# Recurrent block of a two-layer trunk: gate products as 64-row pairs one step later, and the high parts of 12 of 16 input weight tiles loaded by casting transfers

## The chip, the cores and the metric

The kernel runs on one core of one Trainium2 chip. A core has TensorE (PE in the profile, with its weight loads PEld), VectorE (DVE), ScalarE (ACT), GpSimd (POOL), SyncE (SP, which here only issues transfers), and 16 DMA engines that move data between HBM and the on-chip memory. Products are accumulated in PSUM, which has eight banks of 128 partitions by 512 float32. The metric is the device time of one execution in microseconds; before the change the median of three runs is 1560.44 us (1560.33 to 1563.29).

## The reference

A trunk of two layers on 512 positions and 1024 channels. Each layer is half a feed-forward block, a token mixer, and another half feed-forward block; the mixer of layer 0 is recurrent, that of layer 1 a gated spatial one. The change touches the recurrent mixer alone:

```
def rg_lru(x, w_a, b_a, w_x, b_x, lam):
    gate_a = sigmoid(block_diag_linear(x, w_a, b_a))      # 16 heads of 64 x 64
    gate_x = sigmoid(block_diag_linear(x, w_x, b_x))
    log_a = -8.0 * gate_a * softplus(-lam)
    a = exp(log_a);  mult = sqrt(-expm1(2.0 * log_a))
    h[t] = a[t] * h[t-1] + x[t] * gate_x[t] * mult[t]     # a scan over positions

def recurrent_mixer(x, w_in, ...):
    y, r = split(x @ w_in, 2)                             # w_in: 1024 x 2048
    r = causal_depthwise_conv(r, conv_w, conv_b)          # 4 taps
    return (gelu(y) * rg_lru(r, ...)) @ w_out
```

## The kernel before, in words

**Split products.** Float32 products are made of three fast ones: each operand is split into a high part `hi`, which ACT writes by a copy into the float32r type, and a low part `lo`, which DVE writes as operand minus `hi`. The product is hi*hi + hi*lo + lo*hi (`mm3`, L245). For activations the helper `split` does it (its copy shows as L117 of ACT, its subtraction as L108 of DVE, like all uses of these two helpers); for weights the class `Sub` does, into the tiles `whi` and `wlo` of a pool with four buffers of each.

**Steps.** All work is a list `subs` of steps; one step is one weight tile and its products. The loop at the end of `trunk` goes through them in order. In step i it splits the weight tile of step i + 3, runs hooks in the phases `pre`, `mid` and `rest`, issues loads (`load_more`), emits the products, then runs `end`, the step's own `post`, and `late`. So the order of each engine's queue is the order in which this loop emits, and the numbers in hooks and plans set it.

**Weight buffers.** Raw weight tiles of 512 KB are loaded by SP into ten buffers (`RAW_BUFS`, tag `raw`). `load_more` loads on as long as fewer than ten tiles are `live`; a tile stops being live once its low part is written. The output projections use a fast scheme of seven products for eight block products, so most of their weight tiles get a second block added in place by POOL transfers that accumulate (L159).

**The recurrent mixer** (L1201 on). Let c0 to c7 be the eight tiles of 128 channels of r, and y0 to y7 those of y. Products in order: first halves (256 positions) of c0 to c3, then their second halves with the same weights, then c4 to c7 and y0 to y7 with 512 positions each, then the output projection. After each tile of r (`r_post`): ACT copies it from its bank with scale and bias (`rc`), DVE adds three taps, one step later ACT and DVE split the result, and at the end of step g PE makes the two gates (`gate`). The gate weights of two heads lie as a block diagonal in 128 x 128, the rest filled with zeros, so a gate is one `mm3` of 128 rows, into a bank of its own. In step g + 1 ACT takes both banks by sigmoids and makes a tanh (`tl`); in step g + 2 DVE multiplies r with its gate (`pr`). `plan` then places, relative to the first y step y0: exponentials, `a2` and `tl` arithmetic, square roots, scans, the gelu of y, and the product of both (`yh`), which makes the left operand of the output projection in blocks of two tiles (`a` in the profile). The blocks and their sums are split again. The output projection's product groups go in the order P1, P5, P2 for the first pair of row blocks, then the same for the second, into the banks A, C, B.

Of the kernel before, what the change touches and what calls it, by code (L numbers as in the profile page):

```python
# [35 lines left out]
SPLIT_AHEAD = 3  # L36
SLOTS = 56


# [34 lines left out]
def trunk(ctx: ExitStack, tc: tile.TileContext, a: dict, out: bass.AP):  # L74
# [57 lines left out]
    class Raw:  # L132


        halves = False

# [35 lines left out]
    class Sub:  # L172
# [1028 lines left out]
    def recurrent(w_in, w_out, norm):  # L1201
        gates = {}

        def load_gate(name, q):
            g = gates[name, q] = slot(name="gw")
            nc.gpsimd.memset(g, 0.0)
            gv = g.rearrange("p (c j) -> p c j", c=4)
            wv = a[f"rec_gate_{name}_w"][0, q * 8 : (q + 1) * 8].rearrange("(c two) i j -> two i c j", two=2)
            for two in range(2):
                nc.sync.dma_start(out=gv[two * 64 : (two + 1) * 64, :, two * 64 : (two + 1) * 64], in_=wv[two])  # L1210

        def split_gate(name, q):
            gates[name, q] = split(gates[name, q])

        at0 = len(subs)
        y0 = at0 + 12
        for n, (name, q) in enumerate((name, q) for q in range(2) for name in ("a", "x")):
            hook(at0 + (-9,-8,-2,-1)[n], "late", lambda name=name, q=q: load_gate(name, q))
            hook(at0 + (-3,-2,3,4)[n], "mid", lambda name=name, q=q: split_gate(name, q))

        rc, ga, gx, tl, pr, ym = {}, {}, {}, {}, {}, {}

        def r_post(c, ps):
            n = now[0]
            g = n + (2 if c < 4 or c == 6 else 1)
            v = rc[c] = slot(name="rc")
# [7 lines left out]
            def gate():  # L1234
                for name in "ax":
                    pg = bank("gate")
                    wh, wl = gates[name, c // 4]
                    cs = slice((c % 4) * P, (c % 4 + 1) * P)
                    mm3(pg, wh[:, cs], wl[:, cs], hl[0], hl[1], True, True)
                    pss.append(pg)  # L1240
                hl.clear()

            def sigmoids():
                for dst, brow in ((ga, V_GA), (gx, V_GX)):
                    dst[c] = slot(name="g")
                    act(dst[c], pss.pop(0), AF.Sigmoid, bias=vcol(brow + c))
                tl[c] = slot(name="tl")
# [6 lines left out]
            hook(n, "late", taps)  # L1254
            hook(n + 1, "mid", lambda: hl.extend(split(v)))
            hook(g, "end", gate)
# [84 lines left out]
        def mk(c0, post, halves):  # L1341

            raw = raw_of(w_in[:, c0 : c0 + P].rearrange("(k p) c -> p k c", p=P), [P, KD, P])
            st = {}

# [8 lines left out]

            last = lambda: post(st[0])
            if not halves:
# [294 lines left out]
    def vec_rest():  # L1651

        nc.vector.memset(stage[:V_ROWS, :P], 0.0)
        for src, r0, n in rows:
            flat = src.rearrange("h d -> (h d)") if len(src.shape) == 2 else src.rearrange("o h d -> (o h d)")
            nc.gpsimd.dma_start(out=stage[r0 : r0 + n, :P], in_=flat.rearrange("(n p) -> n p", p=P))

# [148 lines left out]
```

## Time and profile before

| | us |
|---|---|
| median of three runs | 1560.44 |
| the profiled execution | 1560.53 |
| its span in the trace | 1558.5 |
| PE busy | 1550.6 |
| DVE busy | 1309.5 |
| ACT busy | 1194.2 |
| POOL busy | 244.5 |
| recurrent products (first r product to first product of the output projection) | 329.46 to 430.50 |

Times within the span are microseconds from its start. Matmuls overlap: one of 512 columns is listed with 0.39 us, but the next starts 0.23 us later, so the start-to-start distance is what a product costs. Likewise an instruction of ACT or DVE starts up to 0.1 us before the one ahead of it ends. A row of the timeline may hold several instructions (x2, x3). The square bracket at its end is the idle time ahead of it and who ended it.

### The profile page before, as it was taken

How to read it: one execution, taken by the hardware profiler on the slowest of the kernel's cores; microseconds unless marked ns; L12 is line 12 of the kernel's file. 1: busy time of each engine (PE TensorE's matmuls, PEld its weight loads, DVE VectorE, ACT ScalarE, POOL GpSimd, SP SyncE). 2: the span in 40 equal slices, each digit the busy share in tenths (PEclk: the TensorE clock that was granted, in tenths of full speed). 3: DMA queues.
4: the chain of work that ended last, by engine and by line, in shares of the span. 5: the costliest groups of instructions: out<-in, count | busy, mean ns of one | idle time of the engine just before them, and what ended most of it. 6: DMA issues, size and time to landing. Idle time of an engine off the chain costs nothing.

```text
span 1558.5 us, 20998 instructions
## 1 busy us (share of the span) xinstructions
PE 1550.6 (99%) x7277; PEld 1317.1 (85%) x7277; DVE 1309.5 (84%) x1784; ACT 1194.2 (77%) x1785; POOL 244.5 (16%) x220
## 2 busy tenths in 40 slices
PE   9999999999999999999999999999999999999998
PEld 7888888898888998888889988888888889888886
DVE  6977789888999787789897877798979997777998
ACT  7877786668778868786787777867987877777856
POOL 2111112300021111112211111122211111111120
PEclk9999999999999999999999999999999999999999
DMA  9888898953395888899987887999978869898994
GB/s 316 187 189 192 188 219 223 232 142 108 98 236 136 191 198 198 187 235 223 232 209 180 191 203 185 230 218 235 252 191 216 203 140 218 197 206 184 241 232 137
DMA packets 272987, 311.58 MB, mean 200 GB/s; under 512 B 115456, under 2 KB 153456, under 8 KB 272880
## 3 DMA queue, kind: packets, MB, share of 16 engines
q1 hardware_dynamic: 218592, 211.06, 46.9%
q0 software_dynamic: 52496, 97.33, 37.1%
q10 hardware_dynamic: 1792, 1.84, 0.4%
q8 instruction: 57, 0.93, 0.2%
q14 instruction: 50, 0.41, 0.1%
HBM read 282.39 MB, written 2.10 MB: 183 GB/s over the span
## 4 chain that ended last, share of the span: by engine, by line
PE 98%; DVE 2%; DMA 0%; issue 0%; ACT 0%; DVEq 0%
PE A L483 15%; PE A L482 15%; PE A L481 15%; PE C L483 8%; PE C L481 8%; PE C L482 8%; PE B L482 4%; PE B L483 4%; PE B L481 4%; PE r L247 2%; PE r L248 2%; PE r L246 2%; PE Q L483 1%; PE Q L481 1%; PE Q L482 1%; PE p L961 1%
## 5 line engine op out<-in xcount | busy, mean ns | idle before, releaser
L108 DVE TENSOR_TENSOR wlo<-raw,whi 128x1024 fp32r<-128x1024 f32 (+2 forms) x567 | 651.1, 1152 | 210.6 <-ACT whi L117 207.0
L117 ACT ACTIVATE whi<-raw 128x1024 fp32r<-128x1024 f32 (+2 forms) x567 | 564.5, 1001 | 229.2 <-DVE raw L108 93.3
L481 PE MATMUL A<-whi,hi 128*128 128x512 f32 (+1 forms) x1104 | 420.8, 381 | 0.0
L482 PE MATMUL A<-whi,lo 128*128 128x512 f32 (+1 forms) x1104 | 419.3, 380 | 0.2 <-DVE lo L108 0.2
L483 PE MATMUL A<-wlo,hi 128*128 128x512 f32 (+1 forms) x1104 | 419.3, 380 | 0.0
L481 PEld LDWEIGHTS A<-whi,hi 128*128 128x128 f32 x1104 | 207.3, 188 | 35.9 <-ACT c L117 1.0
L482 PEld LDWEIGHTS A<-whi,lo 128*128 128x128 f32 x1104 | 207.3, 188 | 35.6 <-DVE lo L108 0.6
L483 PEld LDWEIGHTS A<-wlo,hi 128*128 128x128 f32 x1104 | 207.2, 188 | 35.7
L159 POOL DMA_DIRECT2D raw<-in_ffn_w_in_dram x100 | 120.7, 1207 | 708.8 <-DVE raw L108 322.8
L481 PE MATMUL C<-whi,hi 128*128 128x512 f32 (+1 forms) x608 | 231.5, 381 | 0.0
L483 PE MATMUL C<-wlo,hi 128*128 128x512 f32 (+1 forms) x608 | 231.3, 380 | 0.0
L482 PE MATMUL C<-whi,lo 128*128 128x512 f32 (+1 forms) x608 | 231.3, 380 | 0.0
L159 POOL DMA_DIRECT2D raw<-in_ffn_w_out_dram x73 | 83.8, 1189 | 319.0 <-DVE wlo L108 204.3
L108 DVE TENSOR_TENSOR raw<-raw,raw 128x1024 f32<-128x1024 f32 (+1 forms) x113 | 130.9, 1158 | 1.1
L482 PEld LDWEIGHTS C<-whi,lo 128*128 128x128 f32 x608 | 114.2, 188 | 20.2
L483 PEld LDWEIGHTS C<-wlo,hi 128*128 128x128 f32 x608 | 114.1, 188 | 19.9
L481 PEld LDWEIGHTS C<-whi,hi 128*128 128x128 f32 x608 | 114.1, 188 | 19.8
L117 ACT ACTIVATE c<-A 128x512 f32<-128x512 f32 (+1 forms) x150 | 81.8, 567 | 46.6 <-PE A L483 46.4
L108 DVE TENSOR_TENSOR lo<-a,hi 128x512 fp32r<-128x512 f32 (+1 forms) x180 | 116.3, 653 | 0.7 <-ACT hi L117 0.7
L117 ACT ACTIVATE hi<-a 128x512 fp32r<-128x512 f32 (+1 forms) x180 | 105.5, 596 | 14.4 <-DVE a L108 12.6
L482 PE MATMUL B<-whi,lo 128*128 128x512 f32 (+1 forms) x304 | 115.8, 381 | 0.0
L481 PE MATMUL B<-whi,hi 128*128 128x512 f32 (+1 forms) x304 | 115.7, 381 | 0.0
(190 smaller groups left out, 1973.5 us busy)
## 6 DMA issues: line engine op xcount, KB each, us to landing
raw<-in_ffn_w_in_dram SPq DMA_DIRECT2D x143, 512.0 KB, 5.5
raw<-in_ffn_w_out_dram SPq DMA_DIRECT2D x98, 512.0 KB, 5.7
raw<-in_ffn_w_in_dram POOLq DMA_DIRECT2D x76, 512.0 KB, 7.5
raw<-in_ffn_w_out_dram POOLq DMA_DIRECT2D x58, 512.0 KB, 8.4
raw<-in_ffn_w_in_dram SPq DMA_DIRECT2D x48, 384.0 KB, 4.0
raw<-in_sg_w_in_dram SPq DMA_DIRECT2D x20, 512.0 KB, 8.6
raw<-in_ffn_w_in_dram POOLq DMA_DIRECT2D x24, 384.0 KB, 6.4
raw<-in_rec_w_in_dram SPq DMA_DIRECT2D x16, 512.0 KB, 5.3
```

Source lines behind the costliest of these rows:

```text
L108: nc.vector.tensor_tensor(out=o, in0=x, in1=y, op=op)
L117: nc.scalar.activation(out=o, in_=x, func=f, **k)
L159: nc.gpsimd.dma_start(out=self.v, in_=src, accum_op=ALU.add)
L246: nc.tensor.matmul(ps, wh, xh, start=start, stop=False)
L247: nc.tensor.matmul(ps, wh, xl, start=False, stop=False)
L248: nc.tensor.matmul(ps, wl, xh, start=False, stop=stop)
L481: nc.tensor.matmul(ps, zh, wh, start=fresh and i == 0, stop=False, **k)
L482: nc.tensor.matmul(ps, zl, wh, start=False, stop=False, **k)
L483: nc.tensor.matmul(ps, zh, wl, start=False, stop=end, **k)
L961: nc.tensor.matmul(bank_of(half, s), z, (sub.lo if m == 2 else sub.hi)[:, q, :], start=left[2] == "2" and (h, q, m) == (0, 0, 0), stop=lef ...
```

## The change

**Gates.** The weights of gate a and gate x of two heads now share one 128 x 128 tile: on rows 0 to 63 the first head's a and x side by side, on rows 64 to 127 the second head's x and a. There are no zeros to fill, and two gate tiles are loaded and split where there were four. A gate step is three pairs of products; the first of a pair contracts rows 0 to 63, the second rows 64 to 127, each into a bank of its own with 128 output partitions. Each bank then holds half of gate a and half of gate x, and ACT takes them with four sigmoids of 64 partitions where it took two of 128. For that the bias of gate x is loaded with its halves exchanged. The table `GATE` sets the gate step: 3 steps behind the tile for c0 to c3 and 2 for c4 to c7, where it was 2 for c0 to c3 and c6, and 1 for c4, c5 and c7.

**Weights.** For c4 to c7 and y0 to y7 a tile is loaded twice: raw by SP as before, and into a second buffer of the raw pool by POOL with a cast to float32r. That second tile is the high part; ACT's copy falls away, DVE's subtraction stays. Its buffer is live until the products of its step are emitted. Such a tile needs two free buffers to be loaded.

**Plan.** Some exponentials, square roots and scans stand half a step to one step later.

```diff
+GATE = (3, 3, 3, 3, 2, 2, 2, 2)
...
             self.fetch()
+            if self.cast:
+                self.h = rawp.tile([P, 1024], F32R, tag="raw", name=nm("rawhi")).rearrange("p (k c) -> p k c", k=k)
+                live.add((self, "hi"))
+                nc.gpsimd.dma_start(out=self.h, in_=self.src)
...
             src = self.raw.v
+            if self.raw.cast:
+                self.hi = self.raw.h
+                _, k, c = src.shape
+                self.lo = wp.tile([P, 1024], F32R, tag="wlo", name=nm("wlo")).rearrange("p (k c) -> p k c", k=k)
+                tt(self.lo, src, f32(self.hi), ALU.subtract)
+                self.raw.used()
+                return
...
-        def load_gate(name, q):
-            g = gates[name, q] = slot(name="gw")
-            nc.gpsimd.memset(g, 0.0)
+        def load_gate(q):
+
+            g = gates[q] = slot(name="gw")
             gv = g.rearrange("p (c j) -> p c j", c=4)
...
+            for n, name in enumerate("ax"):
+                wv = a[f"rec_gate_{name}_w"][0, q * 8 : (q + 1) * 8].rearrange("(c two) i j -> two i c j", two=2)
+                for two in range(2):
+                    o = (two ^ n) * 64
+                    nc.sync.dma_start(out=gv[two * 64 : (two + 1) * 64, :, o : o + 64], in_=wv[two])
...
-            g = n + (2 if c < 4 or c == 6 else 1)
+            g = n + GATE[c]
...
             def gate():
-                for name in "ax":
-                    pg = bank("gate")
-                    wh, wl = gates[name, c // 4]
-                    cs = slice((c % 4) * P, (c % 4 + 1) * P)
-                    mm3(pg, wh[:, cs], wl[:, cs], hl[0], hl[1], True, True)
-                    pss.append(pg)
+                pss.extend(bank("gate") for _ in range(2))
+                cs = slice((c % 4) * P, (c % 4 + 1) * P)
+                for m in range(3):
+                    for two in range(2):
+                        rows = slice(two * 64, (two + 1) * 64)
+                        nc.tensor.matmul(pss[two], gates[c // 4][m == 2][rows, cs], hl[0][m == 1][rows, :],
+                                         start=m == 0, stop=m == 2)
                 hl.clear()
 
             def sigmoids():
-                for dst, brow in ((ga, V_GA), (gx, V_GX)):
-                    dst[c] = slot(name="g")
-                    act(dst[c], pss.pop(0), AF.Sigmoid, bias=vcol(brow + c))
+                for dst, brow, n in ((ga, V_GA, 0), (gx, V_GX, 1)):
+                    g = dst[c] = slot(name="g")
+                    for two in range(2):
+                        o = (two ^ n) * 64
+                        act(g[two * 64 : (two + 1) * 64], pss[two][o : o + 64], AF.Sigmoid, bias=vcol(brow + c)[o : o + 64])
...
-        plan(-2, "rest", (exp_, 0, 1, 2, 3, 4), (oma2, 0, 1))
+        plan(-1, "rest", (exp_, 0, 1, 2, 3, 4), (oma2, 0, 1))
...
-        plan(1, "late", (exp_, 5, 6, 7), (oma2, 5, 6, 7))
-        plan(2, "rest", (sqrt, 5, 6, 7))
-        plan(2, "late", (gelu, 0, 1, 2), (scan, 5, 6, 7))
+        plan(2, "rest", (exp_, 5, 6, 7), (oma2, 5, 6, 7))
+        plan(2, "late", (sqrt, 5, 6, 7))
+        plan(2, "late", (gelu, 0, 1, 2))
+        plan(3, "rest", (scan, 5, 6, 7))
...
+            raw.cast = not halves
...
-        while loaded < n and len(live) < RAW_BUFS:
+        while loaded < n and len(live) < RAW_BUFS - raws[loaded].cast:
```

How the queues move is seen at two places. The first is DVE's queue around the taps of c7 (the three rows with 509, 510 and 511 columns; `rc_3768` before, `rc_3746` now). Before:

```order
L108 TENSOR_TENSOR wlo_3724<-raw_3116,whi_3723 128x1024
L108 TENSOR_TENSOR pr_3727<-rc_3524,g_3658 128x512
L108 TENSOR_TENSOR pr_3729<-rc_3580,g_3664 128x512
L108 TENSOR_TENSOR lo_3738<-rc_3718,hi_3737 128x512
L114 SCALAR_TENSOR_TENSOR rc_3768<-r_3743,vec,rc_3768 128x509
L114 SCALAR_TENSOR_TENSOR rc_3768<-r_3743,vec,rc_3768 128x510
L114 SCALAR_TENSOR_TENSOR rc_3768<-r_3743,vec,rc_3768 128x511
```

With the change:

```order
L115 SCALAR_TENSOR_TENSOR rc_3746<-r_3713,vec,rc_3746 128x509
L115 SCALAR_TENSOR_TENSOR rc_3746<-r_3713,vec,rc_3746 128x510
L115 SCALAR_TENSOR_TENSOR rc_3746<-r_3713,vec,rc_3746 128x511
L109 TENSOR_TENSOR wlo_3751<-raw_3566,rawhi_3568 128x1024
L109 TENSOR_TENSOR pr_3753<-rc_3489,g_3681 128x512
L109 TENSOR_TENSOR pr_3755<-rc_3545,g_3689 128x512
L109 TENSOR_TENSOR lo_3766<-rc_3746,hi_3765 128x512
```

The two products `pr` of c3 and c4 with their gates stood ahead of the taps of c7 and now stand behind them.

The second is ACT's queue between the copy of a tile of r from its bank (`rc`) and the exponentials (`g<-g`). Before, this copy is that of c5 and the sigmoids are those of c3 and c4:

```order
L117 ACTIVATE rc_3644<-r_3603,vec 128x512
L117 ACTIVATE whi_3650<-raw_3094 128x1024
L117 ACTIVATE g_3656<-gate_3628,vec 128x512
L117 ACTIVATE g_3658<-gate_3632,vec 128x512
L117 ACTIVATE tl_3660<-g_3656,lru_c 128x512
L117 ACTIVATE g_3662<-gate_3636,vec 128x512
L117 ACTIVATE g_3664<-gate_3640,vec 128x512
L117 ACTIVATE tl_3666<-g_3662,lru_c 128x512
L117 ACTIVATE hi_3668<-rc_3644 128x512
L117 ACT_TABLE_LOAD
```

With the change it is the copy of c6, and the sigmoids are again those of c3 and c4:

```order
L118 ACTIVATE rc_3669<-r_3628,vec 128x512
L118 ACTIVATE g_3678<-gate_3653,vec 64x512
L118 ACTIVATE g_3678<-gate_3654,vec 64x512
L118 ACTIVATE g_3681<-gate_3653,vec 64x512
L118 ACTIVATE g_3681<-gate_3654,vec 64x512
L118 ACTIVATE tl_3684<-g_3678,lru_c 128x512
L118 ACTIVATE g_3686<-gate_3661,vec 64x512
L118 ACTIVATE g_3686<-gate_3662,vec 64x512
L118 ACTIVATE g_3689<-gate_3661,vec 64x512
L118 ACTIVATE g_3689<-gate_3662,vec 64x512
L118 ACTIVATE tl_3692<-g_3686,lru_c 128x512
L118 ACTIVATE hi_3694<-rc_3669 128x512
```

The weight copy `whi` is gone, four sigmoids are eight, and the whole group has moved from behind c5 to behind c6.

More of the change, by code (lines that the diff above doesn't have):

```diff
@@ L132, in trunk @@
     class Raw:
-        halves = False
+        halves = cast = False
         def __init__(self, src, shape, plus=None, wait=2):
@@ L1202, in recurrent, with split_gate @@
         gates = {}
-        def load_gate(name, q):
-            g = gates[name, q] = slot(name="gw")
-            nc.gpsimd.memset(g, 0.0)
+        def load_gate(q):
+            g = gates[q] = slot(name="gw")
             gv = g.rearrange("p (c j) -> p c j", c=4)
[L1208 to L1213, printed above, removed]
+            for n, name in enumerate("ax"):
[3 more added lines that the diff above has]
+                    nc.sync.dma_start(out=gv[two * 64 : (two + 1) * 64, :, o : o + 64], in_=wv[two])
+        def split_gate(q):
+            gates[q] = split(gates[q])
         at0 = len(subs)
         y0 = at0 + 12
-        for n, (name, q) in enumerate((name, q) for q in range(2) for name in ("a", "x")):
-            hook(at0 + (-9,-8,-2,-1)[n], "late", lambda name=name, q=q: load_gate(name, q))
-            hook(at0 + (-3,-2,3,4)[n], "mid", lambda name=name, q=q: split_gate(name, q))
+        for q in range(2):
+            hook(at0 + (-9, -2)[q], "late", lambda q=q: load_gate(q))
+            hook(at0 + (-3, 3)[q], "mid", lambda q=q: split_gate(q))
         rc, ga, gx, tl, pr, ym = {}, {}, {}, {}, {}, {}
@@ L1254, in r_post @@
             hook(n, "late", taps)
-            hook(n + 1, "mid", lambda: hl.extend(split(v)))
+            hook(n + 1, "mid", lambda: hl.append(split(v)))
             hook(g, "end", gate)
@@ L1353, in mm_of, with last @@
                 return mm
-            last = lambda: post(st[0])
+            def last():
+                live.discard((raw, "hi"))
+                post(st[0])
             if not halves:
@@ L1655, in vec_rest @@
             flat = src.rearrange("h d -> (h d)") if len(src.shape) == 2 else src.rearrange("o h d -> (o h d)")
-            nc.gpsimd.dma_start(out=stage[r0 : r0 + n, :P], in_=flat.rearrange("(n p) -> n p", p=P))
+            v = flat.rearrange("(n p) -> n p", p=P)
+            if r0 == V_GX:
+                for o in (0, 64):
+                    nc.gpsimd.dma_start(out=stage[r0 : r0 + n, o : o + 64], in_=v[:, 64 - o : 128 - o])
+            else:
+                nc.gpsimd.dma_start(out=stage[r0 : r0 + n, :P], in_=v)
     def vec_rest_t():
```

1 line of the change is left out of this document (added).

## The prediction

> **What bounds the kernel now.** I read the page first: busy times, then the chain that ended last.
>
> ```profile
> span 1558.5 us, 20998 instructions
> PE 1550.6 (99%) x7277; PEld 1317.1 (85%) x7277; DVE 1309.5 (84%) x1784; ACT 1194.2 (77%) x1785; POOL 244.5 (16%) x220
> PE 98%; DVE 2%; DMA 0%; issue 0%; ACT 0%; DVEq 0%
> ```
>
> PE has work in 99% of the span and makes up the chain, so the time is the sum of the products unless PE starves. The table of stretches says how near that is in the recurrence (329 to 430 us):
>
> ```profile
> core 0: us, PE busy (x) PEld busy (x) DVE busy (x) ACT busy (x) POOL busy (x), PEclk, DMA share, GB/s
> 370.00:380.00 10.00, 10.00 (x46) 8.29 (x45) 7.25 (x10) 9.97 (x16) 0.00 (x0) 1.00 0.57 134
> 400.00:410.00 10.00, 10.00 (x46) 8.29 (x45) 9.83 (x13) 8.86 (x12) 0.00 (x0) 1.00 0.16 52
> 430.00:440.00 10.00, 10.00 (x45) 8.28 (x45) 10.00 (x16) 6.10 (x9) 2.14 (x2) 1.00 1.00 219
> ```
>
> PE never stops, but ACT fills 370 to 380 and DVE fills 400 to 410 and 430 to 440: there is a second engine just behind PE. How far behind is read in the timeline, where the output projection's fifth product group (P5 on the second pair of row blocks, bank C) starts:
>
> ```profile
> 439.13 0.63 ACT L117 ACTIVATE hi<-a 128x512 fp32r<-128x512 f32 x1 [1.18 <-DVE a L108]
> 440.15 0.68 DVE L108 TENSOR_TENSOR lo<-a,hi 128x512 fp32r<-128x512 f32 x1
> 441.38 0.39 PE L481 MATMUL C<-whi,hi 128*128 128x512 f32 x1
> 441.61 0.39 PE L482 MATMUL C<-whi,lo 128*128 128x512 f32 x1
> ```
>
> The low part that PE needs at 441.61 is written by DVE until 440.15 + 0.68 = 440.83. So PE has 0.78 us to spare there. Whatever the change saves on PE before this point is kept only as far as DVE's 440.83 also moves forward.
>
> **The change part by part.**
>
> *Gate products.* Eight tiles of six 128-row products become eight of three pairs, one product on rows 0 to 63 and one on rows 64 to 127, into different banks.
>
> ```profile
> L246 PEld LDWEIGHTS gate<-hi,hi x16: 187/188/192, 351.2 to 391.5; 128*128 128x128 f32 x16
> L246 PE MATMUL gate<-hi,hi x16: 389/389/396, 351.3 to 391.7; 128*128 128x512 f32 x16
> 351.35 0.40 PE L246 MATMUL gate<-hi,hi 128*128 128x512 f32 x1
> 352.73 0.28 PE L246 MATMUL r<-zh,whi 128*128 128x256 f32 x1
> 352.85 0.28 PE L247 MATMUL r<-zl,whi 128*128 128x256 f32 x1
> 355.61 0.40 PE L246 MATMUL gate<-hi,hi 128*128 128x512 f32 x1
> 363.87 0.39 PE L246 MATMUL r<-zh,whi 128*128 128x512 f32 x1
> 369.31 0.39 PE L246 MATMUL gate<-hi,hi 128*128 128x512 f32 x1
> ```
>
> Six gate products take 352.73 - 351.35 = 1.38 us (0.23 each, start to start); 24 products of 512 columns 369.31 - 363.87 = 5.44 (0.227 each); 24 of 256 columns 355.61 - 352.73 = 2.88 (0.12 each). No row shows two 64-row products at once, so their price is bounded: if a pair takes one product's time, 0.227 and 0.68 for three pairs, saving 8 x 0.70 = 5.6 us; if they follow one another, 1.38 and nothing is saved. A pair also needs two weight loads. The 256-column row shows a load keep up with a step of 0.12, so two fit in 0.24: no bar. I take 0.68, because the two share no array rows and no bank, and keep 1.38 for the range. A switch between 128-row and 64-row products may also cost something: at least nothing, at most the part of a product that the next one normally covers, 0.389 - 0.227 = 0.16 us, twice per group of pairs. I take nothing, and keep 0.16.
>
> [...]
>
> *Sigmoids.* Each gate bank now holds half of each gate, so two ACT instructions of 128 partitions become four of 64.
>
> ```profile
> 371.13 1.25 ACT L117 ACTIVATE g<-gate,vec 128x512 f32<-128x512 f32 x2
> 372.27 0.73 ACT L117 ACTIVATE tl<-g,lru_c 128x512 f32<-128x512 f32 x1
> 372.88 1.27 ACT L117 ACTIVATE g<-gate,vec 128x512 f32<-128x512 f32 x2
> 374.64 0.64 ACT L117 ACTIVATE hi<-rc 128x512 fp32r<-128x512 f32 x1
> 375.30 1.28 ACT L117 ACT_TABLE_LOAD   x1
> 376.59 3.18 ACT L117 ACTIVATE g<-g,lru_nc 128x512 f32<-128x512 f32 x5
> 379.68 0.76 ACT L117 ACTIVATE rc<-r,vec 128x512 f32<-128x512 f32 x1
> 380.34 1.05 ACT L117 ACTIVATE whi<-raw 128x1024 fp32r<-128x1024 f32 x1
> 380.47 2.31 DVE L114 SCALAR_TENSOR_TENSOR rc<-r,vec,rc 128x509 f32<-128x509 f32 x3 [0.38 <-ACT rc L117]
> 383.83 1.29 DVE L108 TENSOR_TENSOR pr<-rc,g 128x512 f32<-128x512 f32 x2
> 385.80 2.32 DVE L114 SCALAR_TENSOR_TENSOR rc<-r,vec,rc 128x509 f32<-128x509 f32 x3
> ```
>
> One sigmoid costs (372.27 - 371.13) / 2 = 0.57, the tanh behind it 0.61. With half the partitions it costs 0.29 if time goes with all elements, 0.57 if with the columns of a partition. I take 0.57, since an ACT copy of 256 columns and all partitions is shorter than one of 512, and no row shows that partitions matter:
>
> ```profile
> L117 ACT ACTIVATE zh<-xt,vec 128x256 fp32r<-128x256 f32 x6 | 2.4, 478 | 0.0
> ```
>
> Sixteen more sigmoids are 9.1 us of ACT; the twelve copies that the casts replace (1.05 at 380.34) give back at most 12.6. In sum that is even, but not in place: ten of the sixteen come before c7's tap, where ACT is full (9.97 of 10 from 370 to 380), and most of the copies that leave stood where it was not.
>
> *Where this ends.* I follow the new order from the last place that the change leaves alone, 351.35 on PE. Second half of c3: 354.23. Pairs of c0: 354.91. c4, pairs of c1, c5, pairs of c2, c6: 360.35, 361.03, 366.47, 367.15, 372.59. ACT takes c6 from its bank 0.2 later (0.66), then the eight half sigmoids and two tanhs of c3 and c4 (8 x 0.57 + 2 x 0.61 = 5.78), the high part of c6 and the table load (375.30 - 374.64 + 1.29 = 1.95), five exponentials (379.68 - 376.59 = 3.09), then c7. It starts c7 at 372.79 + 0.66 + 5.78 + 1.95 + 3.09 = 384.27, and DVE's first tap of c7 follows 0.79 later (380.47 - 379.68), at 385.06. Before, that tap stood at 385.80. So of 5.6 us on PE, 0.7 reach DVE's queue at this point.
>
> ```profile
> 419.54 0.69 DVE L108 TENSOR_TENSOR lo<-a,hi 128x512 fp32r<-128x512 f32 x1 [0.36 <-ACT hi L117]
> ```
>
> From that tap to the low part above DVE took 440.83 - 385.80 = 55.03 us, with no break longer than this 0.36. The change leaves the same instructions between the two, and two more: the products of c3 and c4 with their gates, done before the tap at 383.83, now stand behind it, since the gates come a step later. They cost 2 x 0.60 = 1.2. One short wait for c7's high part (0.2 as I count ACT's queue) comes on top. The low part is ready at 385.06 + 55.03 + 1.4 = 441.5, against 441.61 when PE needed it before. PE's products before it would allow 441.61 - 5.6 = 436.0; it waits for DVE, and what it gains in the whole run is 441.61 - 441.5 = 0.1 us. I see nothing behind that point that differs.
>
> *Gate weights.* Two slots less to fill and split: four memsets of POOL, two splits, one instruction each on ACT and DVE, ahead of 346, where both have idle time. Nothing:
>
> ```profile
> 340.00:350.00 10.00, 10.00 (x85) 10.00 (x85) 7.15 (x14) 5.72 (x12) 0.00 (x0) 1.00 0.04 10
> ```
> The vector of biases takes one more small POOL transfer of 0.5 us near 37 us; PE is not short there.
>
> *Casting transfers.* Twelve of 512 KB, POOL's queue, with rows of 512 B.
>
> ```profile
> q1 hardware_dynamic: 218592, 211.06, 46.9%
> q0 software_dynamic: 52496, 97.33, 37.1%
> raw<-in_rec_w_out_dram POOLq DMA_DIRECT2D x8, 512.0 KB, 7.2
> 367.38 1.21 POOL L159 DMA_DIRECT2D raw<-in_rec_w_out_dram  x1 [59.82 <-DMA raw<-in_rec_w_out_dram]
> L1656 POOL DMA_DIRECT2D stage<-in_rec_lambda_dram x1: 497/497/497, 41.3 to 41.3; - x1
> 350.00:360.00 10.00, 10.00 (x62) 8.84 (x61) 8.87 (x13) 8.26 (x12) 0.00 (x0) 1.00 0.42 124
> ```
>
> No cast is in the trace. POOL spends 0.50 on a few rows and 1.21 on 256; with 1024 rows that is 0.50 + 4 x 0.71 = 3.3, at most 4 x 1.21 = 4.8, at least 1.2. On the DMA engines 0.524 MB costs 1.8 us by q1's share and 3.1 by q0's (whose transfers also add), 22 to 37 us in all, in stretches used to 0.2 to 0.6. To landing I take 7.2. What it must beat: two buffers a tile leave five tiles in flight, so those of y2 come free when PE ends c4 (360.4), and DVE wants them behind c6's taps, near 376: 15 us for 3.3 + 7.2. Hidden. POOL's adds for the output weights stand behind all twelve casts, but PE's tiles come every 6.1 us (5.44 + 0.68) and POOL needs at most 4.8.
>
> Sum: the profiled execution took 1560.53 us, its span and 2.0 around it, the median of the runs 1560.44. Less 0.1 gives **1560.4 us**.
>
> **The rivals.**
>
> *Faster: the queue of ACT is lighter than I count.* If a half sigmoid costs 0.29, c7's tap comes 8 x 0.28 = 2.2 earlier and the gain is 2.3; if DVE's breaks ahead of c7 close as well, up to 5.6: 1554.8 to 1558.1. For it: ACT loses twelve copies. Against: c3 and c4 are still done in one piece ahead of the exponentials. Chance 0.16, nearly all below 1557.3.
>
> *No overlap: the change doesn't do what it says.* Pairs take 1.38, so c6 ends 3 x 0.70 = 2.1 later, and so does the low part: 441.5 + 2.1 against 441.61, 1562.4. Chance 0.15.
>
> [...] Chance 0.12.
>
> *Slower: casts arrive late.* Place: POOL's queue, which is in order. If a cast holds POOL for more than 6.1 us, or lands more than 12 us after issue, DVE stops at the low part of a y tile, and the adds of the output weights come as much later. At 7 us a cast, six more y tiles put it 5 us back: 1565, more if slower still. For it: 1024 rows, priced from 256. Against: a margin of some 5 us. Chance 0.12.
>
> **How the numbers follow.** Forecast, pairs overlap and DVE holds the gain: 0.45, within 1558.5 to 1562. A measurement of this kernel can tell about 0.2%, 3.1 us, from no change: below 1557.3 is faster, above 1563.6 slower. Faster: 0.15 of the first rival. Slower: 0.12 of the casts, 0.05 of the drains and 0.06 for waits of this size that I did not find. Same: the rest, 0.62. The range 1557.0 to 1564.5 takes in no overlap, the drains and the light half of the first rival, and leaves out its best part and casts that are more than 4 us late.
>
> **What would show it.** Right: gate products in pairs that start within some 0.02 us; sigmoids of 64 partitions near 0.69 each; PE idle of 3 to 6 us between 405 and 442, released by DVE, most of it at the C group; DVE's low part for that group near 441.5. Wrong: gate pairs with 0.23 between starts; half sigmoids near 0.35; DVE or PE waiting for the casting transfers; the C group starting 2 us or more before 441.

## The result and the profile after

The change makes the kernel slower by 0.2%: a median of 1563.45 us over 15 runs against 1560.54 us over 15 runs of the kernel before, ratio 1.002 with a 95% interval of 1.0013 to 1.0026. The forecast was 1560.4 us, a gain of 0.1 and so no measurable change; instead 2.9 us are lost, more than the interval leaves to chance. The time does lie inside the stated range, 1557.0 to 1564.5, but that range was drawn to take in other ways of coming out, pairs that do not overlap and switches of the array that cost time; the sum that gave 1560.4 is refuted all the same. The profiled execution took 1564.33 us. Medians, here and below, leave out one execution of 1936.85 us, at a granted clock of 0.75, of the kernel with another order of half sigmoids.

The page of the kernel after, span and busy times:

```profile
span 1562.5 us, 21029 instructions
PE 1549.9 (99%) x7277; PEld 1311.5 (84%) x7277; DVE 1308.6 (84%) x1782; ACT 1194.8 (76%) x1787; POOL 253.6 (16%) x229
```

The busy times hardly moved: ACT has the same 1194 us although twelve copies left it. The timeline shows where the 4.0 us of the span arise. First the C group that the prediction spoke of, in the kernel after:

```profile
424.83 0.50 PE L260 MATMUL r<-zh,wlo 128*128 128x512 f32 x1 [2.08 <-DVE wlo L109]
442.87 0.51 PE L493 MATMUL C<-whi,hi 128*128 128x512 f32 x1 [1.72 <-ACT hi L118]
443.21 0.68 DVE L109 TENSOR_TENSOR lo<-a,hi 128x512 fp32r<-128x512 f32 x1
443.95 0.50 PE L494 MATMUL C<-whi,lo 128*128 128x512 f32 x1 [0.57 <-DVE lo L109]
445.05 0.63 PE L495 MATMUL C<-wlo,hi 128*128 128x512 f32 x1
448.03 0.52 PE L493 MATMUL B<-whi,hi 128*128 128x512 f32 x1
```

and the end of the same group in the kernel before:

```profile
444.11 0.39 PE L481 MATMUL B<-whi,hi 128*128 128x512 f32 x1
```

The low part is ready at 443.21 + 0.68 = 443.89, not at 441.5 as forecast, nor at 440.83 as before. PE waits for it (and, earlier, 2.08 us at y7, the last input tile). Its second C product starts at 443.95 instead of 441.61, 2.34 later. From there to the first product of the next group, bank B, it needs 448.03 - 443.95 = 4.08 instead of 444.11 - 441.61 = 2.50. That second loss was in no term of the sum. The table of stretches of the kernel after shows it:

```profile
core 0: us, PE busy (x) PEld busy (x) DVE busy (x) ACT busy (x) POOL busy (x), PEclk, DMA share, GB/s
444.00:445.00 1.00, 1.00 (x4) 0.81 (x5) 1.00 (x2) 1.00 (x2) 0.00 (x0) 0.94 1.11 209
445.00:446.00 1.00, 1.00 (x4) 0.76 (x3) 1.00 (x3) 0.24 (x1) 0.67 (x1) 0.50 1.18 211
447.00:448.00 1.00, 1.00 (x3) 0.74 (x3) 1.00 (x3) 0.11 (x1) 0.00 (x0) 0.50 1.08 240
448.00:449.00 1.00, 1.00 (x5) 0.84 (x4) 1.00 (x2) 0.96 (x1) 0.00 (x0) 0.85 1.11 252
```

Right after the wait the granted clock (the number behind the five engines) falls to 0.50 for some 3.4 us, and a product takes 0.63 instead of 0.39. So B's first product is 3.92 later than before, and the rest of the program is as long as it was (1562.5 - 448.03 = 1114.5, before 1114.4). This moment, the start of the first B product behind the C group, is the measure of the experiments below: 444.11 before, 448.03 after.

Two cautions go with it. The profiled executions reach the first r product between 328.9 and 329.5 (329.46 before, 329.02 after), so a difference of this moment between two kernels is good to some 0.5 us. And from it to the end they take 1114.4 to 1117.1 us: seven of the runs below have a wait of PE of about 1 us, in two of them split in two, at a product group near 720, 1036 or 1520, far behind the change, and the kernel before and the change have none there. A median can hold such waits too, so it is the less sharp of the two measures.

Why the low part is late is read backwards, on ACT and DVE of the kernel after:

```profile
359.10 2.81 ACT L118 ACTIVATE g<-gate,vec 64x512 f32<-64x512 f32 x4
361.94 0.72 ACT L118 ACTIVATE tl<-g,lru_c 128x512 f32<-128x512 f32 x1
373.66 0.78 ACT L118 ACTIVATE rc<-r,vec 128x512 f32<-128x512 f32 x1 [1.20 <-PE r L260]
374.55 2.81 ACT L118 ACTIVATE g<-gate,vec 64x512 f32<-64x512 f32 x4
378.01 2.78 ACT L118 ACTIVATE g<-gate,vec 64x512 f32<-64x512 f32 x4
381.45 0.62 ACT L118 ACTIVATE hi<-rc 128x512 fp32r<-128x512 f32 x1
382.09 0.69 DVE L109 TENSOR_TENSOR lo<-rc,hi 128x512 fp32r<-128x512 f32 x1 [3.57 <-ACT hi L118]
387.25 2.32 DVE L115 SCALAR_TENSOR_TENSOR rc<-r,vec,rc 128x509 f32<-128x509 f32 x3 [0.38 <-ACT rc L118]
391.99 0.61 ACT L118 ACTIVATE hi<-rc 128x512 fp32r<-128x512 f32 x1
392.63 0.69 DVE L109 TENSOR_TENSOR lo<-rc,hi 128x512 fp32r<-128x512 f32 x1 [0.73 <-ACT hi L118]
```

Four half sigmoids take 361.94 - 359.10 = 2.84, 0.71 each from start to start; two whole ones took 1.14. ACT works without a break from 374.55 to 391.99 + 0.61 = 392.60, and in that time DVE stands still for 3.57 us once and for shorter times later. From 392.63 on DVE has a full queue (two breaks of 0.36) and reaches the low part at 443.21.

The pairs on PE, in the kernel after, around the gates of c1:

```profile
360.12 0.39 PE L260 MATMUL r<-zh,wlo 128*128 128x512 f32 x1
360.44 0.50 PE L1254 MATMUL gate<-hi,hi 64*128 64x512 f32 x2
360.77 0.40 PE L1254 MATMUL gate<-lo,hi 64*128 64x512 f32 x2
361.00 0.40 PE L1254 MATMUL gate<-hi,lo 64*128 64x512 f32 x2
361.33 0.50 PE L258 MATMUL r<-zh,rawhi 128*128 128x512 f32 x1
361.67 0.40 PE L259 MATMUL r<-zl,rawhi 128*128 128x512 f32 x1
```

Two products of a pair share one row, the first row 0.50 long with each of its two products 0.49: they start within 0.01 us and do run side by side. But four steps are longer than 0.23: 0.32 into the group, 0.33 behind its first pair, 0.33 out of it, 0.34 behind the first 128-row product. A group costs (361.33 - 360.12 - 0.23) + (0.34 - 0.23) = 1.09, not 0.68; 0.41 of it is the switch there and back. Against 1.38 before, a group saves 0.29.

### The profile page after: what moved, and what is told of

The parts are those of the page before. It is cut to its first block, busy times and chain, and to the rows that moved or that the text cites. A ratio compares the mean times of both kernels' runs of the same rounds, so it can differ in the third digit from the quotient of the medians.

```text
span 1562.5 us, 21029 instructions
## 1 busy us (share of the span) xinstructions
PE 1549.9 (99%) x7277; PEld 1311.5 (84%) x7277; DVE 1308.6 (84%) x1782; ACT 1194.8 (76%) x1787; POOL 253.6 (16%) x229
## 4 chain that ended last, share of the span: by engine, by line
PE 92%; DVE 4%; ACT 1%; DMA 1%; issue 1%; SPq 0%; DVEq 0%
PE A L494 15%; PE A L493 15%; PE A L495 15%; PE C L494 8%; PE C L495 8%; PE C L493 8%; PE B L494 4%; PE B L495 4%; PE B L493 4%; PE Q L493 1%; PE Q L494 1%; PE Q L495 1%; PE p L973 1%; DVE wlo L109 1%; PE r L258 1%; PE r L259 1%
## 5 line engine op out<-in xcount | busy, mean ns | idle before, releaser
L109 DVE TENSOR_TENSOR wlo<-raw,whi 128x1024 fp32r<-128x1024 f32 (+2 forms) x555 | 636.7, 1151 | 211.1 <-ACT whi L118 208.9
L118 ACT ACTIVATE whi<-raw 128x1024 fp32r<-128x1024 f32 (+2 forms) x555 | 551.8, 1000 | 230.9 <-DVE raw L109 94.0
```

The source lines that it names most:

```text
L109: nc.vector.tensor_tensor(out=o, in0=x, in1=y, op=op)
L118: nc.scalar.activation(out=o, in_=x, func=f, **k)
```

## The experiments

The theory after this reading: ACT's half sigmoids hold up DVE, DVE holds up PE at the C group, and a PE that has waited may lose clock. Rivals: the switches of the array cost the time by themselves; the casting transfers cost it.

| kernel | median us | ratio to before (95%) | first B product |
|---|---|---|---|
| the change | 1563.45 | 1.0020 (1.0013 to 1.0026) | 448.03 |
| whole sigmoids | 1559.40 | 0.9987 (0.9979 to 0.9996) | 442.95 |
| ten fillers at C | 1564.82 | 1.0025 (1.0015 to 1.0034) | 447.86 |
| casts alone | 1560.07 | 0.9993 (0.9984 to 1.0002) | 443.73 |
| pairs alone | 1572.62 | 1.0069 (1.0056 to 1.0081) | 455.19 |
| fillers at y7 and C | 1563.51 | 1.0022 (1.0014 to 1.0031) | 446.71 |
| other order of pairs | 1564.29 (one run) | | 446.76 |
| other order of half sigmoids | 1563.73 | 1.0020 (1.0011 to 1.0030) | 448.25 |
| products on POOL | 1561.57 | 1.0008 (0.9999 to 1.0017) | 444.98 |
| squares on ACT | 1559.71 | 0.9995 (0.9987 to 1.0004) | 442.96 |
| the same, fewer switches | 1558.92 | 0.9988 (0.9979 to 0.9997) | 442.52 |
| exponentials later | 1564.93 | 1.0025 (1.0014 to 1.0035) | 446.94 |
| before, with the relief | 1562.29 | 1.0004 (0.9995 to 1.0013) | 444.03 |

Medians are over 5 to 15 executions, but for the one run. Ratios are those of the comparison with the kernel before in the same session, whose medians lay between 1560.5 and 1561.1; they are the recorded estimates and not plain quotients of the medians.

**Whole sigmoids.**

```
-                for dst, brow, n in ((ga, V_GA, 0), (gx, V_GX, 1)):
-                    g = dst[c] = slot(name="g")
-                    for two in range(2):
...
+                for dst, brow in ((ga, V_GA), (gx, V_GX)):
+                    dst[c] = slot(name="g")
+                    act(dst[c], pss.pop(0), AF.Sigmoid, bias=vcol(brow + c))
```

> The change with one sigmoid of 128 partitions per gate bank in place of two halves (two ACT instructions a tile, 16 in all, instead of 32). This kernel leaves the sorting of the halves out: each gate tile holds half of one gate and half of the other. Theory (ACT's queue delays DVE, DVE delays the C group, and the idle PE then loses clock): a half sigmoid takes 0.71 from start to start, a whole one 0.57, so each tile takes 4 x 0.71 - 2 x 0.57 = 1.7 less on ACT, 3.4 of it for c3 and c4 just ahead of c7's first tap; the low part for the C group comes 1.5 to 3 us earlier than in the change, PE waits under 1.2 there, its clock stays at 1.00 between 444 and 449, and the time is 1559.5 to 1561. Rival (switches between 64-row and 128-row products cost the time by themselves): 1563, as the change. Rival (the casting transfers cost it): 1563, with waits for raw tiles.

ACT and the C group of this kernel:

```profile
374.94 1.26 ACT L118 ACTIVATE g<-gate,vec 128x512 f32<-128x512 f32 x2
388.86 0.68 DVE L109 TENSOR_TENSOR lo<-rc,hi 128x512 fp32r<-128x512 f32 x1
439.57 0.69 DVE L109 TENSOR_TENSOR lo<-a,hi 128x512 fp32r<-128x512 f32 x1
427.97 0.39 PE L493 MATMUL A<-whi,hi 128*128 128x512 f32 x1
```

The low part comes 3.64 earlier than in the change (the theory said 1.5 to 3), PE waits 0.8 at C and nowhere at y7, no stretch of the recurrence or of the output projection's first groups shows a lower clock, and the time is 4 us below the change's: 1559.40, just under the range named. Nothing on PE or in the transfers differs, so ACT's half sigmoids decide; both rivals fall as the main cause. The last row also gives what the pairs are worth to PE where it does not wait: the output projection's first product starts at 427.97, at 430.50 before. That is 2.53, not 5.6; eight groups less seven switches (the gates of c3 and c4 follow one another), 8 x 0.70 - 7 x 0.41, give 2.7.

**Casts alone, pairs alone.** The first is the kernel before with `raw.cast = not halves` and what it needs, the second the change without that line.

> The kernel before with the casting transfers alone: gates stay as six products of 128 rows with the old steps. Theory: the casts harm nothing and relieve ACT by 12 x 1.05 us, but PE, which is the bound there, has nothing to gain: 1560.0 to 1560.8, no wait of PE between 350 and 460, clock 1.00. Rival (casts and the two buffers that they take cost the time): 1562 to 1564, with PE or DVE waiting for raw tiles.

> The change without the casting transfers: pairs, half sigmoids and later steps as in the change, high parts by ACT as before. Theory (ACT's queue): ACT has 12 copies of 1.05 us more, some six of them between 351 and 387 where it was busy 9.5 of 10 already, so c7's tap and the low part of the C group come about 6 us later than in the change, with waits of PE at y tiles as well: 1567 to 1572. Rival (the casts cost the time): 1558 to 1561. Rival (the switches of the products alone): 1563 to 1564, since ACT does not matter.

Casts alone change nothing that can be measured, and PE waits nowhere between 340 and 480. Pairs alone cost 0.7%; PE waits where ACT's copies are late (view of waits, PE, 340 to 480):

```profile
engine line waited for: us in total, times, longest us
PE r L258 <- ACT whi L118: 3.1, 2, 1.8
PE gate L1254 <- ACT hi L118: 1.9, 1, 1.9
PE r L260 <- DVE wlo L109: 1.0, 2, 0.5
```

So the casting transfers are not the harm but what pays for the half sigmoids: without them the change would lose 11.6 us against the median before, not 2.9. The range named, 1567 to 1572, was 0.6 too low.

**Fillers in PE's waits.** Products of zeros, added to the bank that PE is about to use:

```
+                    for _ in range(10 if now[0] == S.fill and s == 0 else 0):
+                        nc.tensor.matmul(ps, warm[:, :P], warm, start=False, stop=False, skip_group_check=True)
```

> The change with ten products of zeros (bf16, 512 columns, some 0.23 us each) that PE adds to bank C right ahead of the C group, where it would wait 1.72 and 0.57 us. Nothing that DVE or ACT does moves. Theory (the wait itself costs 2.3 us, and the fall of the granted clock to 0.50 that follows it another 1.7): the second C product starts where it did, within 0.3 of 443.95, but the clock stays at 1.00 between 444 and 449, C to B takes 2.5 instead of 4.08, and the time is 1561.5 to 1562. Rival (the clock falls for another reason, or its fall is only in the records): 1563.4 as the change, and the fall at 445 stays.

Neither theory was right. The fall at 445 was gone, but now there was one at y7, behind the wait of 2.08 us that in the change had left the clock alone (stretches of this kernel):

```profile
427.00:428.00 1.00, 1.00 (x4) 0.71 (x4) 1.00 (x2) 1.00 (x2) 0.00 (x0) 0.50 0.89 334
428.00:429.00 1.00, 1.00 (x4) 0.81 (x3) 1.00 (x2) 1.00 (x3) 0.00 (x0) 0.50 0.27 90
```

PE so reached the C group later, and ten fillers were too many there: the second C product started at 445.35. The next kernel filled both waits, with nine products at y7 and seven at C.

> The change with PE kept busy in both of its waits: nine products of zeros between the second and the third product of y7 (there PE waited 2.08 us for DVE's low part), and seven ahead of the C group instead of the ten of the run before, which were about 1.4 us too many after the clock had already fallen at y7. Theory (idle PE loses clock, at one of the two waits or the other): the clock is 1.00 in every stretch of 10 us from 420 to 460, the second C product starts within 0.3 of 443.95, because DVE sets it and DVE is as before, C to B takes 2.5, and the span is 1560.7 to 1561.3 against 1562.5 of the profiled execution of the change; the median is at most 1 us below the change's 1563.45. Rival (the half clock does not come from idle time): a fall to about 0.8 in one of these stretches stays.

```profile
420.00:430.00 10.00, 9.79 (x43) 7.04 (x43) 9.24 (x17) 5.17 (x8) 0.00 (x0) 1.00 0.77 219
440.00:450.00 10.00, 9.21 (x39) 6.45 (x39) 10.00 (x15) 5.34 (x8) 3.62 (x3) 1.00 1.06 244
446.71 0.39 PE L495 MATMUL B<-whi,hi 128*128 128x512 f32 x1
```

The clock stays at 1.00, and B starts at 446.71, 1.32 earlier than in the profiled execution of the change. PE waits 0.6 here, where the change waits 4.4, and the fall is gone with the waits: here it is idle time that takes the clock. But the median stays, 1563.51. The mean granted clock of every execution is on record: 0.998 in all 15 of the change, 0.999 or 1.0 in all 11 of this kernel; 3.4 us at 0.50 are 1.7 of 1562 us, 0.001. So the change had about one such fall in every execution, and taking it away gained nothing in the median. The other order of pairs (below) explains it as far as the profiles go: it had its fall at y7, and B at 446.76. A fall at y7 costs nothing, because PE would otherwise wait for DVE at C; only a fall at C costs. So DVE's lateness alone makes B 2.6 to 2.7 later, which is most of the 2.9 of the medians, and the clock's 1.3 to 1.6 belongs to the profiled execution of the change. Where it fell in the executions without a profile is not recorded.

**Another order of the pairs.**

```
-                for m in range(3):
-                    for two in range(2):
+                for two in range(2):
+                    for m in range(3):
```

> The change with the six gate products of a tile in another order: the three on rows 0 to 63 first, then the three on rows 64 to 127, so that neighbours no longer use different halves of the array. If pairs run side by side in the change: here 0.23 from start to start for most of the six, and the group takes about 0.7 longer than in the change, where its three pairs start 0.34 and 0.23 apart. If the 64-row products cost half of a 128-row one for another reason (shorter weights): the same length as in the change.

```profile
354.02 0.51 PE L1254 MATMUL gate<-hi,hi 64*128 64x512 f32 x2
354.36 0.40 PE L1254 MATMUL gate<-lo,hi 64*128 64x512 f32 x2
354.60 0.40 PE L1254 MATMUL gate<-hi,lo 64*128 64x512 f32 x2
354.92 0.50 PE L258 MATMUL r<-zh,rawhi 128*128 128x512 f32 x1
```

The first reading expected 0.7 more; the group takes 0.90 to the next 128-row product, in the change 0.89. The rows, where x2 stands for two products, still show couples, although each product's partner now stands three places behind it in the program. So a product on one row half did not wait here for those ahead of it in the program on the other half. The order within a group of pairs made no difference, and the run does not test overlap as I had meant it to; the couples of the trace and the length of a group do show it.

**Another order of the half sigmoids.**

> The change with the four half sigmoids of a tile in another order: first the two that read partitions 0 to 63 of the banks, then the two that read 64 to 127. Theory A (the 0.71 from start to start is the price of one ACT instruction on its own, which only the next one on the same partitions can overlap): the steps inside each couple fall to about 0.57, the group from 2.81 to about 2.5, and the time falls by 0.5 to 1 us. Theory B (instructions of 64 partitions do not overlap at all): 0.71 in every step, 1563.4.

Theory B holds, and the time is that of the change: the four of c0 start at 358.95 and the tanh behind them at 361.78, still 0.71 each. Sharing input partitions with the neighbour is not what lets two sigmoids overlap. Why those of 64 partitions do not overlap (0.68 long, 0.71 apart), and those of 128 do (0.69 long, 0.57 apart), stays open.

**Which link of the chain.** The prediction hung the low part on the moment of c7's first tap. This kernel moves that moment alone:

```
-        plan(-1, "rest", (exp_, 0, 1, 2, 3, 4), (oma2, 0, 1))
+        plan(0, "pre", (exp_, 0, 1, 2, 3, 4), (oma2, 0, 1))
```

> The change with the five exponentials (with their table load, 4.5 us of ACT) issued behind the taking of c7 from its bank, not ahead of it; nothing else. c7's first tap on DVE comes some 4 us earlier than in the change (387.25). Theory A, as the prediction had it (the time from c7's tap to the C group's low part is fixed, and the tap's moment sets the end): low part some 4 us earlier, 1559 to 1560. Theory B (DVE is held by its whole queue, work and waits for ACT together, and an earlier tap only moves its wait to the squares behind the exponentials): the low part within 1 us of the change's 443.2, time 1562.5 to 1564.

```profile
383.12 2.32 DVE L115 SCALAR_TENSOR_TENSOR rc<-r,vec,rc 128x509 f32<-128x509 f32 x3
392.35 0.61 ACT L118 ACTIVATE hi<-rc 128x512 fp32r<-128x512 f32 x1
393.00 0.69 DVE L109 TENSOR_TENSOR lo<-rc,hi 128x512 fp32r<-128x512 f32 x1 [2.57 <-ACT hi L118]
443.56 0.68 DVE L109 TENSOR_TENSOR lo<-a,hi 128x512 fp32r<-128x512 f32 x1
```

The kernel before, c7's low part:

```profile
389.76 0.69 DVE L108 TENSOR_TENSOR lo<-rc,hi 128x512 fp32r<-128x512 f32 x1
```

The tap is 4.13 earlier, the low part 0.35 later. DVE's wait at c7's low part grew from 0.73 to 2.57 in its place. ACT does the same work in another order and ends c7's high part at 392.96 instead of 392.60, and from c7's low part to the C group's it is 443.56 - 393.00 = 50.56, in the change 443.21 - 392.63 = 50.58. Before the change it is 440.15 - 389.76 = 50.39. With whole sigmoids, where c7's low part starts 3.77 earlier than in the change, it is 439.57 - 388.86 = 50.71, so there the end did move with it. The link is c7's high part, the last thing that DVE waits for, but for the two breaks of 0.36.

The time of this run, 1564.93, is above both ranges named, by 0.9 for theory B. Up to B it is no slower than the change (446.94 against 448.03, its fall of the clock being at y7); behind B its profiled execution waits 1.0 at a C group near 719.

**Relief for DVE.** If DVE's queue is what PE waits for, a shorter queue must give the pairs' gain back. A first try put the eight products of gate and branch on POOL, let DVE make the high parts of c4 to c6 itself, and moved the sum S1 and its split for the second pair of row blocks a step ahead (`(s1, 1)` from step 9 to 8, its split from 10 to 9).

> The change with work taken from DVE and moved within its queue, nothing changed on PE: the eight products of gate and branch (pr) on POOL, the high parts of c4, c5 and c6 on DVE where it waits for ACT, and for the second pair of row blocks the sum S1 and its split one step earlier, ahead of low parts of weights that are needed later. Theory (DVE's queue from c7's tap to the C group is what PE waits for): of about 57 us 3 go to POOL and 1 to 2 us of waits close, so PE waits under 1.2 at C and not at all at y7, the clock stays 1.00, and the time is 1558.5 to 1560, below the kernel before by what the pairs save on PE less the switches (about 2). [...]

```profile
368.00 2.48 DVE L110 TENSOR_TENSOR lo<-rc,hi 128x512 fp32r<-128x512 f32 x1
368.62 1.30 POOL L1271 TENSOR_TENSOR pr<-rc,g 128x512 f32<-128x512 f32 x1
402.63 2.13 DVE L1298 TENSOR_TENSOR_SCAN h<-g,pr 128x512 f32<-128x512 f32 x1
```

Half a success, 1561.57, above the range named: beside a product of POOL (368.62 to 369.92) a DVE subtraction takes 2.48 instead of 0.69, and beside another (402.05 to 403.69) a scan 2.13 instead of 1.22 (a third instruction, a product, takes 1.71 instead of 0.67), so some of the 3 us return as longer instructions of DVE. The trace shows DVE held up beside a product of POOL, by these 1.8 and 0.9 us; DVE's subtraction starts 0.62 before POOL's product, and what holds it up the trace does not show. The second try gave the products back to DVE, kept the rest, and used ACT, which in the change is busy for 5.62 of the 10 us from 410 to 420:

```
-            tt(a2[c], ga[c], ga[c], ALU.mult)
+            act(a2[c], ga[c], AF.Square) if c in (5, 6, 7) else tt(a2[c], ga[c], ga[c], ALU.mult)
```

> The change with DVE relieved without POOL, whose tensor instruction of the last run held up DVE: the squares of the gates of c5, c6 and c7 as ACT instructions (3 x 0.6 us less on DVE in the stretch that PE waits for), the high parts of c4, c5, c6 on DVE (0.42 each, where it waited for ACT), S1 and its split of the second pair a step earlier. Products on PE as in the change. Theory (the end of DVE's queue at the C group sets the loss): no wait at y7, at most 0.8 at C, clock 1.00, span 1556.5 to 1558, time 1558.3 to 1559.8, so 0.7 to 2.2 below the kernel before. Rival (switches of the array cost more than the pairs save): 1561 or more with no wait left on PE.

> The run with squares on ACT, and the gates of c1 and of c3 one step earlier, so that the pairs of c0 and c1 stand together, and those of c2 and c3, with no 128-row products between: five or six groups instead of seven. Theory (a switch to 64 rows and back costs some 0.4 us a group, by the starts in the change: 0.10 to 0.11 at four places): 0.4 to 0.8 less than the run with squares on ACT, as long as the earlier gates do not have to wait for their low parts. If the low parts are late: the same or more.

> The kernel before, without the change, with the same relief of DVE as the run with squares on ACT. Theory (before, PE was the bound and waited for nobody in the recurrence, so an emptier DVE is worth nothing): 1560.0 to 1561.0, same as before. If the relief by itself is worth something: below 1559.5, and the gain of the run with squares on ACT is then not the pairs'.

With the squares on ACT, y7's wait is gone, one of 0.96 is left at C (at most 0.8 was expected), and B starts at 442.96. The span, 1560.1, was above the range named: that execution has one of the waits far behind, 1.2 at a C group near 716. The median, 1559.71, is inside the range, though its ratio does not tell it from the kernel before.

The last kernel has the same relief and the gates of c1 and c3 a step earlier, in the order `GATE = (3, 2, 3, 2, 2, 2, 2, 2)`, so six groups instead of seven. Its PE around the first joined group, and the first B product:

```profile
354.65 0.39 PE L1255 MATMUL gate<-hi,lo 64*128 64x512 f32 x2
354.87 0.40 PE L1255 MATMUL gate<-hi,hi 64*128 64x512 f32 x2
356.70 0.47 PE L259 MATMUL r<-zh,rawhi 128*128 128x512 f32 x1 [0.98 <-issue]
442.52 0.39 PE L494 MATMUL B<-whi,hi 128*128 128x512 f32 x1
```

No switch lies between the two groups (0.22), and PE does not wait at C at all: its first product there starts at 439.80 with the low part ready at 439.04. It is faster than the kernel before, if by little, at 0.9988 (0.9979 to 0.9997) of its time, an interval that lies below that of the change as well, despite a wait of 0.98 behind the joined group and one of 0.50 near 370 that the closer gates brought. How much of the 0.8 us to the run before it is the switch saved, and how much DVE, whose low part now is ready in time, this run does not separate.

The kernel before with the same relief gains nothing: its B starts at 444.03, without the relief at 444.11, and its ratio is 1.0004 (0.9995 to 1.0013). Its median, 1562.29, is above the range named; in its profiled execution PE waits 1.4 and 0.5 at the Q group near 1520, and whether the relief has to do with that is not shown. Casts alone have B at 443.73. So the earlier B of the last two kernels, 442.96 and 442.52, is in the main the pairs', once DVE lets PE keep it.

## Why the prediction was wrong, step by step

The step that failed is the sum from the second half of c3 to the low part of the C group, by two terms of about the same size: the switch, taken as nothing, put c6's end 3 x 0.41 = 1.23 later, and the half sigmoid, taken as 0.57 from start to start, measured 0.71, 8 x 0.14 = 1.12 on ACT. What bounds the kernel, that pairs overlap, and that the casts stay hidden was right.

- *What bounds the kernel.* Right. The C group was the tightest place, PE waited there for DVE, and the time follows when that low part is ready. PE's idle time between 405 and the C group, 2.08 + 1.72 + 0.57 = 4.4 us (the last of it ends at 443.95), is within the 3 to 6 named, but hardly more than half of it is at C, the rest at y7.
- *Gate products, 0.68 a group, a switch taken as nothing.* Overlap was right, the switch was not: 0.41 a group, above the bound of 2 x 0.16. The bound held only the tail that the next product covers, and the rows show longer steps on both sides of each switch. What PE does in these longer steps the trace does not show. PE gained 2.53 where it did not wait, not 5.6.
- *Half sigmoid, taken as 0.57.* The other term that failed. A whole sigmoid is 0.69 long and its neighbour starts after 0.57; a half is 0.68 long and its neighbour starts after 0.71. The step of 0.57 was taken from a couple of whole ones, and whether halves overlap was never asked. The bounds, 0.29 to 0.57, did not hold 0.71. The halves themselves cost more than this missed 0.14: for c3 and c4 whole sigmoids need 4 x 0.57 = 2.3 where the halves need 8 x 0.71 = 5.7, and the prediction had counted 8 x 0.57 = 4.6.
- *The chain to the low part, 441.5.* It came at 443.89, and the 2.4 split up: c6 is taken at 373.66, not 372.79 (+0.87: three groups of pairs are 1.23, and this execution reached the recurrence 0.44 earlier than the one before, 329.02 against 329.46); the first sigmoid follows 0.23 later than counted, since it waits for its gate's products (the last pair of c3's gates starts at 374.12 and is listed with 0.40); sigmoids and tanhs of c3 and c4 take 381.45 - 374.55 = 6.90, not 5.78 (+1.12); 0.2 is left behind the tap. No further term was needed because ACT works through without a break. The anchor of the sum was wrong: moving the tap by 4.13 did not bring the low part forward, and c7's high part, counted as a short wait, is the true link.
- *"I see nothing behind that point that differs."* Wrong for the profiled execution: a fall of the clock to 0.50 for some 3.4 us, 1.58 between the second C product and bank B. In the medians, by the fillers, it hardly counts.
- *Casting transfers hidden.* Right, at a lower price. The group of the kernel after:

```profile
L154 POOL DMA_DIRECT2D rawhi<-in_rec_w_in_dram x12 | 10.6, 880 | 76.1 <-DVE wlo L109 39.9 <-PE r L260 19.0 <-DVE lo L109 17.2
```

  POOL spends 0.88 each, not 3.3. No wait of PE or DVE for a raw tile is in the trace, and casts alone are 0.9993 (0.9984 to 1.0002).
- *"In sum that is even, but not in place."* Half right: with 0.71 the halves cost 4 x 0.71 - 1.14 = 1.7 a tile, 13.6 in all, against 12.6 of copies.
- *Rivals.* "Faster" fell with the half sigmoid, "no overlap" with the couples of the trace, "casts late" with POOL's 0.88. The chances also name drains, 0.12 for them and 0.05 within "slower"; no run shows a drain, and what the runs show in its place is the longer steps at a switch, 0.41 a group. At the bound of 0.16, two switches a group and three groups ahead of c6's end, overlapping pairs would have come to 1560.4 + 1.0 = 1561.4. That switches cost time was so true and too cheap; the result is their real price plus the mis-sized sigmoid, a combination that had no line of its own.
- *What a measurement can tell, 0.2% or 3.1 us.* Too wide: the interval here reaches from 1.0013 to 1.0026, about 0.07% to either side. By the limit of 1563.6 that followed from it, this result would not have counted as slower.

## What to carry to other kernels

Cutting an instruction in two on an engine that runs just behind the bound is priced by start-to-start steps of the halves, and these need not overlap as the wholes did (here 0.71 against 0.57). When the bound engine gets faster, look for the last wait of the engine that feeds it: here part of what PE saved reached the end only after that queue was shortened, and the same shortening was worth nothing before the change. A moment that precedes the end by a fixed time is a link only if moving it alone moves the end.

## What the runs showed of the hardware

- Products on rows 0 to 63 and on rows 64 to 127 formed couples even where they stood three places apart in the program (other order of pairs: starts 354.02, 354.36 and 354.60, two each); a switch from 128 rows to 64 and back costs 0.41 us a group (the change, gates of c1).
- After one wait of PE of 1.72 and one of 0.57 close together (the change), or one of 2.08 (ten fillers at C), the granted clock fell to 0.50 for some 3.4 us. With a wait of 2.1 in the other order of pairs and with the exponentials later, its mean over 420 to 430 was 0.83, as with ten fillers at C. Which of two such waits does it differs between executions of nearly the same program: the one at C in the change, the one at y7 in the other order of pairs. Filled with products of zeros, neither does (1.00). Waits of 1.8 and 1.0 us, with the products on POOL, left the clock at 1.00. What sets the length of the fall, and which wait brings it, no run shows.
- Sigmoids of ACT on 64 partitions follow one another at 0.71 us (the change), those on 128 at 0.57 (the kernel before), for the same 512 columns.
